# Stick-breaking attention: order of the projections, delays of copies, engine of the low parts, and place of the returns

## The chip, the cores and the metric

The kernel runs on one core of one Trainium2 chip. The core has five engines that each work through their own list of instructions in order: TensorE (PE) multiplies matrices, VectorE (DVE) and ScalarE (ACT) work on whole tiles, GpSimd (POOL) does the same and also issues DMAs here, and SyncE (SP) only issues DMAs. The metric is the time of one execution on the device in microseconds (us), smaller is better. Two kernels are compared by the median of several runs.

## The reference

One sequence of 1024 tokens, 1024 channels wide, in float32, passes two layers. Layer 0 mixes tokens with a gated linear recurrence, layer 1 with stick-breaking attention; a SwiGLU feed-forward follows each, with RMSNorm ahead of every part. The change lies in the attention of layer 1, 16 heads of 64 channels:

```
qkv = x @ w_qkv                                # (S, 3, 16, 64)
z = q @ k.T / 8                                # per head
log_fail = where(s < t, log_sigmoid(-z), 0)
suffix = cumsum(log_fail, reverse) - log_fail
weights = where(s < t, exp(log_sigmoid(z) + suffix), 0)
o = weights @ v
out = concat(o) @ w_o
```

So a query gives each earlier key a share of what the keys between the two have left over.

## The kernel before

Float32 products are made from two parts: a tile is split in a high part in a shorter format (a copy on ACT) and a low part, the difference (a subtraction on DVE or POOL), and `mm3` (lines 142 to 145) multiplies high by high, high by low and low by high.

Attention is lines 1473 to 1887. Heads go in eight pairs `q`, since two heads fill 128 partitions. For each pair the generator `qkv_steps` (line 1562) makes three projections, `which` 0, 1 and 2 for queries, keys and values, each in two halves `n` of 512 tokens. A half is eight steps of three matmuls, so a pair takes 48 steps. `next_weights` (line 1547) splits the weights of the projection after the present one, and `column_norms` (line 1525) finds scale factors `sv` and `av_` from the value weights, the last two operations of which are on POOL (lines 1541 and 1542).

`evacuate` (line 1589) takes a finished half out of its PSUM bank. Queries: a copy on ACT into `two`, a subtraction for the low part, and four DMAs from POOL (`spread`) that lay the parts out per head in `Q`. Keys: a multiplication on DVE into `t`, then the same, four DMAs into `KK`. Values: a product (line 1599) and a difference `t` (line 1601) on DVE, then `high` on ACT (line 1619) and `low` on DVE (line 1606) into `vx`, and two transposing DMAs from SP into `VV`. Differences of neighbouring values are used because the weights are kept as running products.

The scores of a head are made in twelve chunks, eight on the diagonal and four off it (`chunk_list`, line 1658). `z_part` multiplies, with two score banks in `psZ`; `z_rest` takes the sigmoid on ACT (line 1680); `scan` forms the running product on DVE (line 1687 on the diagonal, line 1690 off it, where it reads two inputs). The four chunks off the diagonal go through `turn_weights` (line 1694): a copy on ACT (line 1697) and a subtraction on POOL (line 1698) make the two f16 parts in `wx`, and a DMA from SP transposes them into `T`, tile name `wt`. The weights on the diagonal are instead transposed on PE (`t_part`) and split by `t_split` (lines 1721 and 1722). `av_part` multiplies weights and values in twelve units a head, one key block each.

After the last unit of a half, `gather`, `add_v` (on POOL, line 1751, except for the last pair) and `parts` bring a pair's outputs to `oo` and split them. They go to DRAM (`store`), because the tiles `xh` and `xl` still hold the projections' input. When the projections are done, `bring_back` (line 1512) loads them into `xh` and `xl` with DMAs from POOL, and the output projection (`ob`, by `out_fill`) begins among the last units.

The order of the work is written out by hand. A loop over `u` from -10 to 191 (line 1842) walks the units. In each, it first does what stands in `soon` (by `due`), then a chunk's scores, the weights of the chunk before (`turning`), the unit itself, one task from `later`, and two projection steps from `fill`. 42 steps are made ahead of the loop (AHEAD is 8), and in eight units of the last quarter only one step is made:

```
slower = range(132, 132 + 4 * AHEAD, 4)
...
                if u >= -2:
                    for _ in range(1 if u in slower else 2):
                        next(fill, None)
```

A function put in `soon` runs at the start of the next unit; there is no longer delay than that, only chains of functions that each put the next one in. The projections end at unit 164. The first twelve returns are issued in the low part of the last pair's first half of values, the other fourteen at the end of `all_fill` (line 1786).

Of the kernel before, what the change touches and what calls it, by code (L numbers as in the profile page):

```python
# [14 lines left out]
ALU = mybir.AluOpType  # L15
PSUM = bass.MemoryType.PSUM

P = 128
S = 1024
D = 1024  # L20
# [14 lines left out]
def trunk(  # L35
# [93 lines left out]
    def cols(w, c0, n=P):  # L129
        return w[:, c0 : c0 + n].rearrange("(k p) c -> p k c", p=P)  # L130
# [1357 lines left out]
    with ExitStack() as st:  # L1488
# [27 lines left out]


        def load_link(i):
            q, which = divmod(i, 3)
            if q < NP:  # L1520
                raws[i] = load_raw(cols(w_qkv, which * D + q * P), (ND,))
            else:
                mix[0].load(which)

        def column_norms(raw, q):
# [3 lines left out]
            def sums():  # L1529
                n_ps = psZ.tile([P, NB], F32, tag="z", name="n_ps")[:, 0:1]  # L1530
                for k in range(ND):
                    nc.tensor.matmul(
                        n_ps, lhsT=sq[:, k], rhs=g2[:, k : k + 1], start=k == 0, stop=k == ND - 1
                    )

                n2, h = (ap.tile([P, 1], t, tag=x, name=x, bufs=2) for x, t in (("n2", F32), ("nh", I32)))
                sv[q], av_[q] = (ap.tile([P, 1], I32, tag=x, name=x, bufs=3) for x in ("sv", "av"))
                nc.vector.tensor_scalar(n2, n_ps, 1e-30, 2.0, op0=ALU.max, op1=ALU.mult)
                one = float(1 << 23)
                nc.vector.tensor_single_scalar(h, n2.bitcast(I32), 24, op=ALU.logical_shift_right)  # L1540
                nc.gpsimd.tensor_scalar(sv[q], h, -one, 213 * one, op0=ALU.mult, op1=ALU.add)
                nc.gpsimd.tensor_scalar(av_[q], h, one, 41 * one, op0=ALU.mult, op1=ALU.add)

# [18 lines left out]
        def qkv_steps(q):  # L1562
            for which in range(3):
# [12 lines left out]
                for n in range(NH):  # L1576
                    pool, tag = (psZ, "z") if (q, which) == (0, 0) else (psQ, "qk")
                    ps = pool.tile([P, NB], F32, tag=tag, name="qk_ps")
                    for i, k in enumerate(ks):
                        mm3(ps, w[0][:, k], w[1][:, k], xh[k][n], xl[k][n], i == 0, i == ND - 1)  # L1580
                        if i < ND - 1:
                            yield
                    ev = evacuate(q, which, n, ps)
                    next(ev)
# [4 lines left out]
        def evacuate(q, which, n, ps):  # L1589
            full = lambda tag, m: [ap.tile([P, m, S], F32R, tag=tag, name=tag, bufs=4 if m == 1 else 3) for _ in range(2)]  # L1590
            cs = slice(n * NB, (n + 1) * NB)
            if which == 2:
# [12 lines left out]
                def low():  # L1605
# [3 lines left out]
                    for hx, a in enumerate((top, bot)):  # L1609
# [4 lines left out]
                        )  # L1614
                    if q == NP - 1 and n == 0:
                        bring_back(*((p, 0) for p in range(NP - 2)))

                def high():
                    nc.scalar.activation(vx[:, :, 0], t3, AF.Copy, scale=1 / UP)
                    soon.append(low)  # L1620

                soon.append(high)
                return
# [11 lines left out]
            def low():  # L1635
                nc.vector.tensor_sub(two[:, 1], t, f32(two)[:, 0])
                soon.append(spread)

# [7 lines left out]
            else:  # L1646
# [4 lines left out]
                yield  # L1651
                nc.scalar.copy(two[:, 0], t)
                soon.append(low)

# [39 lines left out]
        def turn_weights(q, hx, j, ci, c0, c1, diag):  # L1694
            F = W[q, hx, j, ci].rearrange("p (b c) -> p b c", c=P)
            wx = ap.tile([P, 4, 2, P], F16, tag="wx", name="wx", bufs=3)
            nc.scalar.copy(wx[:, :, 0], F)
            nc.gpsimd.tensor_sub(wx[:, :, 1], F, wx[:, :, 0])
            if j == 4:
# [27 lines left out]
        def av_part(tht, q, hx, G, kb, first, last):  # L1727
# [25 lines left out]
            def parts():  # L1753
# [9 lines left out]
                else:  # L1763
# [6 lines left out]

                    soon.append(store)

# [6 lines left out]
        units = [u for q, hx in heads for u in unit_list(q, hx)]  # L1779
        LEAD, AHEAD = 10, 8  # L1780

        def all_fill():
            yield from first
            for q in range(1, NP):
                yield from qkv_steps(q)
            bring_back((NP - 2, 0), *((p, 1) for p in range(NP - 2)))

# [21 lines left out]
        with tc.manual_schedule(engines={E.PE, E.Activation, E.DVE, E.Pool, E.SP}):  # L1809
# [11 lines left out]
            def due():  # L1821
                now = soon[:]
                soon.clear()
                for task in now:
                    task()

# [8 lines left out]
            gains = [len(units) - x for x in (31, 29, 27)]  # L1835
            slower = range(132, 132 + 4 * AHEAD, 4)

# [4 lines left out]
            for u in range(-LEAD, len(units)):  # L1842
# [28 lines left out]
                if u >= -2:  # L1871
                    for _ in range(1 if u in slower else 2):
                        next(fill, None)
# [60 lines left out]
```

## Time and profile before

| | |
|---|---|
| median of 3 runs | 2181.56 us (2178.86 to 2181.8) |
| the profiled execution | 2182.57 us |
| its span in the trace | 2179.8 us |
| mean granted clock of TensorE | 0.992 |
| attention in the trace | about 966 to 1460 us |
| DMA traffic over the span | 315.47 MB |

The span runs from the first to the last record of the trace; the profiled execution's own time has a little around it. In the lines of the profile, L1698 is line 1698 of the kernel. `out<-in` gives the tiles by their names in the program. A row of a timeline has the start, the duration, the engine, the line, the operation, its tiles and shapes, how many were merged, and in brackets how long the engine stood idle before it and who ended that wait. A wait line has the waiting engine and line, the one waited for, the total, the number of times and the longest. PEclk is the clock granted to TensorE, 1.00 at full speed. A busy time can hold time in which the instruction was held up.

### The profile page before, as it was taken

What the parts mean: (1) busy time and instruction counts of PE and PEld (TensorE: products, weight loads), DVE (VectorE), ACT (ScalarE), POOL (GpSimd) and SP (SyncE); (2) the same over time, 40 slices, a digit from 0 to 9 for tenths busy, and PEclk for the clock granted to TensorE, in tenths of its full rate; (3) what the DMA queues carried; (4) which work ended last, traced back from release to release, by engine and by line L of the source; (5) the groups of instructions that cost most, each with busy time, mean ns of one, the idle gap of its engine ahead of it and who ended that gap; (6) DMA issues with size and microseconds to landing.
All of it is one profiled execution on the core that took longest, in us unless ns stands there. A gap on an engine that the chain in (4) does not pass through costs nothing.

```text
span 2179.8 us, 28179 instructions
## 1 busy us (share of the span) xinstructions
PE 2137.5 (98%) x10158; PEld 1747.9 (80%) x10158; DVE 1769.7 (81%) x2543; ACT 1133.0 (52%) x1838; POOL 315.9 (14%) x346
## 2 busy tenths in 40 slices
PE   8999999999999999999999999889999999999998
PEld 7888888888888888887777777668888888888887
DVE  7888778888888887887888788866888888888886
ACT  6667445443444544555655555543544444454556
POOL 1222020000000000013444444531000000000002
PEclk9999999999999999999999999989999999999999
DMA  7111422344445864446676656873133444587452
GB/s 233 49 49 39 161 88 73 105 126 160 136 156 200 268 218 124 150 129 149 138 155 138 129 134 141 205 213 124 58 108 120 154 141 153 171 275 237 137 154 91
DMA packets 380844, 315.47 MB, mean 145 GB/s; under 512 B 101272, under 2 KB 296992, under 8 KB 380704
## 3 DMA queue, kind: packets, MB, share of 16 engines
q1 hardware_dynamic: 368192, 274.60, 42.2%
q0 software_dynamic: 12352, 38.81, 7.0%
q8 instruction: 79, 1.29, 0.2%
q14 instruction: 61, 0.50, 0.1%
q10 hardware_dynamic: 160, 0.27, 0.0%
HBM read 184.09 MB, written 83.36 MB: 123 GB/s over the span
## 4 chain that ended last, share of the span: by engine, by line
PE 90%; DVE 4%; issue 2%; DMA 2%; ACT 2%; POOL 1%; SPq 0%; DVEq 0%; ACTq 0%; POOLq 0%
PE p_ps L143 17%; PE p_ps L145 17%; PE p_ps L144 17%; PE qk_ps L143 3%; PE qk_ps L144 3%; PE qk_ps L145 3%; PE a_ps L144 3%; PE a_ps L145 3%; PE a_ps L143 3%; PE ob_ps L145 3%; PE ob_ps L143 2%; PE ob_ps L144 2%; PE av_ps L1735 2%; PE i_ps L145 1%; PE i_ps L144 1%
## 5 line engine op out<-in xcount | busy, mean ns | idle before, releaser
L143 PE MATMUL p_ps<-vh,wbh 128*128 128x512 f32 x524 | 204.9, 391 | 0.0
L144 PE MATMUL p_ps<-vl,wbh 128*128 128x512 f32 x524 | 204.5, 390 | 0.0
L145 PE MATMUL p_ps<-vh,wbl 128*128 128x512 f32 x524 | 204.0, 389 | 0.2 <-DVE wbl L726 0.2
L143 PE MATMUL p_ps<-vh,wch 128*128 128x512 f32 x524 | 204.2, 390 | 0.0
L145 PE MATMUL p_ps<-vh,wcl 128*128 128x512 f32 x524 | 204.1, 389 | 0.0
L144 PE MATMUL p_ps<-vl,wch 128*128 128x512 f32 x524 | 203.9, 389 | 0.0
L722 ACT CAST wbh<-sb 128x1024 fp32r<-128x1024 f32 (+2 forms) x69 | 69.6, 1009 | 192.6 <-DVE sb L702 192.6
L1680 ACT ACTIVATE w<-z_ps,rs 128x128 f32<-128x128 f32 (+1 forms) x192 | 110.1, 581 | 99.1 <-PE z_ps L1668 86.7
L143 PE MATMUL p_ps<-vh,wah 128*128 128x512 f32 x396 | 154.0, 389 | 0.0
L144 PE MATMUL p_ps<-vl,wah 128*128 128x512 f32 x396 | 154.0, 389 | 0.0
L145 PE MATMUL p_ps<-vh,wal 128*128 128x512 f32 x396 | 154.0, 389 | 0.0
L218 POOL TENSOR_TENSOR acc<-acc,rbc 128x512 f32<-128x512 f32 x30 | 40.6, 1352 | 766.8 <-ACT rbc L217 766.8
L1687 DVE TENSOR_TENSOR_SCAN w<-w,unit 128x128 f32<-128x128 f32 (+3 forms) x128 | 117.3, 923 | 21.9 <-ACT w L1680 21.8
L145 PEld LDWEIGHTS p_ps<-vh,wbl 128*128 128x128 f32 x524 | 98.4, 188 | 21.6 <-DVE wbl L726 0.7
L145 PEld LDWEIGHTS p_ps<-vh,wcl 128*128 128x128 f32 x524 | 98.4, 188 | 21.0 <-DVE wcl L736 0.6
L143 PEld LDWEIGHTS p_ps<-vh,wch 128*128 128x128 f32 x524 | 98.4, 188 | 20.5 <-ACT tb L1181 0.2
L144 PEld LDWEIGHTS p_ps<-vl,wch 128*128 128x128 f32 x524 | 98.4, 188 | 20.4
L143 PEld LDWEIGHTS p_ps<-vh,wbh 128*128 128x128 f32 x524 | 98.6, 188 | 19.8 <-ACT U L1181 0.4
L144 PEld LDWEIGHTS p_ps<-vl,wbh 128*128 128x128 f32 x524 | 98.6, 188 | 18.5
L143 PE MATMUL qk_ps<-vh,whi 128*128 128x512 f32 x264 | 113.2, 429 | 0.0
L1722 DVE TENSOR_TENSOR tl<-wt_ps,th 128x512 f16<-128x512 f32 (+3 forms) x128 | 56.6, 483 | 61.6 <-ACT th L1721 61.6
L144 PE MATMUL qk_ps<-vl,whi 128*128 128x512 f32 x264 | 104.6, 396 | 0.0
(411 smaller groups left out, 6073.7 us busy)
## 6 DMA issues: line engine op xcount, KB each, us to landing
raw<-in_ffn_w_in SPq DMA_DIRECT2D x88, 512.0 KB, 4.1
vl<-pd SPq DMA_DIRECT2D x128, 256.0 KB, 3.7
pd<-U SPq DMA_DIRECT2D x90, 256.0 KB, 2.3
kk<-two POOLq DMA_DIRECT2D x64, 256.0 KB, 4.6
raw<-in_ffn_w_out SPq DMA_DIRECT2D x56, 256.0 KB, 3.6
raw<-in_attn_w_qkv SPq DMA_DIRECT2D x24, 512.0 KB, 5.9
h<-hd SPq DMA_DIRECT2D x32, 256.0 KB, 5.5
hd<-h SPq DMA_DIRECT2D x32, 256.0 KB, 2.0
```

Source lines behind the costliest of these rows:

```text
L143: nc.tensor.matmul(ps, lhsT=wh, rhs=mh, start=first, stop=False, **kw)
L144: nc.tensor.matmul(ps, lhsT=wh, rhs=ml, start=False, stop=False, **kw)
L145: nc.tensor.matmul(ps, lhsT=wl, rhs=mh, start=False, stop=last, **kw)
L218: (eng or nc.gpsimd).tensor_add(acc[n], acc[n], sq)
L722: nc.scalar.copy(self.full(self.wb), self.full(self.sb))
L1680: nc.scalar.activation(F, ps[:, 0:n], AF.Sigmoid, scale=rs[:, j : j + 1])
L1687: nc.vector.tensor_tensor_scan(rev, rev, unit[:, NB - n :][:, ::-1], 0.0, op0=ALU.mult, op1=ALU.add)
L1722: nc.vector.tensor_sub(tl[:, q0:], tp[:, q0:], th[:, q0:])
L1735: nc.tensor.matmul(ps[:, q0:], lhsT=VV[q][:, hx, kb], rhs=t[:, q0:], start=first and x == 0, stop=last and x == 1)
```

## The change

From the second pair on, a pair's projections come in the order keys, queries, values (`kind`). `stage(task, steps)` puts a task into `soon` with a delay in units, and `due` counts it down. The keys' copy on ACT comes one unit later, the values' copy two units after their difference is formed, and the two POOL operations for `sv` and `av_` two units after the sums. In `turn_weights` the subtraction goes from POOL to DVE. The returns are taken out of `all_fill`: the first twelve are issued one unit after the low part of the first half of the last values, the other fourteen two units after that of the second half. AHEAD is 4, so 38 steps are made ahead of the loop, and `slower` is gone; the projections end at unit 162.

```diff
+        def kind(q, i):
+            return i if q == 0 else (1, 0, 2)[i]
+
+        def stage(task, steps=1):
+            soon.append([steps, task])
...
-                raws[i] = load_raw(cols(w_qkv, which * D + q * P), (ND,))
+                raws[i] = load_raw(cols(w_qkv, kind(q, which) * D + q * P), (ND,))
...
-                nc.gpsimd.tensor_scalar(sv[q], h, -one, 213 * one, op0=ALU.mult, op1=ALU.add)
-                nc.gpsimd.tensor_scalar(av_[q], h, one, 41 * one, op0=ALU.mult, op1=ALU.add)
+
+                def factors():
+                    nc.gpsimd.tensor_scalar(sv[q], h, -one, 213 * one, op0=ALU.mult, op1=ALU.add)
+                    nc.gpsimd.tensor_scalar(av_[q], h, one, 41 * one, op0=ALU.mult, op1=ALU.add)
+
+                stage(factors, 2)
...
-                    ev = evacuate(q, which, n, ps)
+                    ev = evacuate(q, kind(q, which), n, ps)
...
-                    if q == NP - 1 and n == 0:
-                        bring_back(*((p, 0) for p in range(NP - 2)))
+                    if q == NP - 1:
+                        back = [(p, n) for p in range(NP - 2)]
+                        stage(lambda: bring_back(*([(NP - 2, 0)] * n + back)), 1 + n)
...
                     nc.scalar.activation(vx[:, :, 0], t3, AF.Copy, scale=1 / UP)
-                    soon.append(low)
-
-                soon.append(high)
+                    stage(low)
+
+                stage(high, 2)
...
-                nc.scalar.copy(two[:, 0], t)
-                soon.append(low)
+
+                def high():
+                    nc.scalar.copy(two[:, 0], t)
+                    stage(low)
+
+                stage(high)
...
-            nc.gpsimd.tensor_sub(wx[:, :, 1], F, wx[:, :, 0])
+            nc.vector.tensor_sub(wx[:, :, 1], F, wx[:, :, 0])
...
-        LEAD, AHEAD = 10, 8
+        LEAD, AHEAD = 10, 4
...
-            bring_back((NP - 2, 0), *((p, 1) for p in range(NP - 2)))
...
-                for task in now:
-                    task()
+                for steps, task in now:
+                    if steps > 1:
+                        stage(task, steps - 1)
+                    else:
+                        task()
...
-            slower = range(132, 132 + 4 * AHEAD, 4)
...
-                    for _ in range(1 if u in slower else 2):
+                    for _ in range(2):
```

More of the change, by code (lines that the diff above doesn't have):

```diff
@@ L1636, in low @@
                 nc.vector.tensor_sub(two[:, 1], t, f32(two)[:, 0])
-                soon.append(spread)
+                stage(spread)
             if which == 0:
@@ L1769, in store @@
                         nc.gpsimd.dma_start(od[q, G][1], o)
-                    soon.append(store)
+                    stage(store)
             later.insert(0, gather)
```

## The prediction

> **What bounds the kernel now.** I read the page's busy times first, then the same by stage, then the waits of TensorE (PE) in one stage, then the timelines around two of those waits.
>
> ```profile
> PE 2137.5 (98%) x10158; PEld 1747.9 (80%) x10158; DVE 1769.7 (81%) x2543; ACT 1133.0 (52%) x1838; POOL 315.9 (14%) x346
> ```
>
> ```profile
> 0.00:966.00 966.00, 958.44 (x4428) 799.34 (x4429) 796.03 (x1130) 505.18 (x728) 66.10 (x39) 1.00 0.43 138
> 966.00:1460.00 494.00, 464.77 (x2350) 349.69 (x2349) 389.98 (x537) 278.55 (x548) 222.68 (x287) 0.97 0.67 150
> 1460.00:2179.80 719.80, 714.28 (x3383) 598.88 (x3381) 583.71 (x876) 349.28 (x563) 27.14 (x20) 1.00 0.46 150
> ```
>
> The windows' columns are stretch, length, busy time of PE, PEld, DVE (VectorE), ACT (ScalarE), POOL (GpSimd), then granted clock, DMA share and GB/s. PE is the bound everywhere, and the change touches only the middle row, attention: there PE is idle for 494.00 - 464.77 = 29.2 us and runs at a mean clock of 0.97. No PE work is added or removed, so the most that can come back is that idle time and what the clock takes. The waits of PE by releaser, up to 1398 us and behind it:
>
> ```profile
> PE z_ps L1667 <- ACT w L1680: 9.6, 7, 2.9
> PE av_ps L1735 <- DVE tl L1722: 1.9, 6, 0.4
> PE av_ps L1735 <- ACT th L1721: 1.5, 4, 0.4
> ...
> PE av_ps L1735 <- DMA wt<-wx: 0.5, 1, 0.5
> ```
>
> ```profile
> PE av_ps L1735 <- DMA v<-vx: 8.0, 1, 8.0
> PE z_ps L1667 <- ACT w L1680: 3.5, 1, 3.5
> PE z_ps L1667 <- DMA kk<-two: 2.3, 1, 2.3
> PE av_ps L1735 <- ACT th L1721: 0.7, 1, 0.7
> ```
>
> So 13.5 us are small waits that come back once per pair of heads, and 14.5 us are three large ones in the last 60 us. The granted clock falls in six stretches:
>
> ```profile
> 1220.40:1223.80 3.40, 3.40 (x12) 2.65 (x11) 3.40 (x8) 1.32 (x4) 0.00 (x0) 0.56 0.52 101
> 1278.50:1281.80 3.30, 2.85 (x9) 1.92 (x9) 3.06 (x6) 2.56 (x7) 0.96 (x1) 0.55 0.36 70
> 1336.50:1343.20 6.70, 5.50 (x14) 3.89 (x15) 4.74 (x10) 4.75 (x11) 1.16 (x1) 0.53 0.40 76
> 1397.90:1401.30 3.40, 2.84 (x10) 2.36 (x11) 3.29 (x5) 0.74 (x2) 3.16 (x5) 0.56 1.05 218
> 1415.00:1421.80 6.80, 4.87 (x13) 3.55 (x14) 3.79 (x7) 4.97 (x12) 3.60 (x7) 0.53 0.91 275
> 1428.70:1438.80 10.10, 4.37 (x14) 2.85 (x15) 7.58 (x8) 3.28 (x7) 3.12 (x3) 0.52 0.77 163
> ```
>
> PE was busy 11.75 us in the first three and 12.1 us in the last three; at about half speed, half of that is lost: 5.9 and 6.0 us. All that can be won is 13.5 + 14.5 + 5.9 + 6.0 = 40 us, 1.8% of the span. Each such stretch follows a wait of PE, so I take the lost clock to go with the waits.
>
> **The wait of each pair.** From ACT's, PE's, DVE's and POOL's timelines:
>
> ```profile
> 1276.83 0.63 ACT L1619 ACTIVATE vx<-t 128x512 f16<-128x512 f32 x1 [3.19 <-DVE t L1601]
> 1277.77 0.45 PE L1667 MATMUL z_ps<-kk,q 128*128 128x384 f32 x1 [1.42 <-ACT w L1680]
> ```
>
> ```profile
> 1266.13 1.27 DVE L1690 TENSOR_TENSOR_SCAN w<-w,w 128x512 f32<-128x512 f32 x1
> 1269.78 2.63 DVE L1690 TENSOR_TENSOR_SCAN w<-w,w 128x512 f32<-128x512 f32 x1
> 1273.57 2.04 DVE L1690 TENSOR_TENSOR_SCAN w<-w,w 128x512 f32<-128x512 f32 x1
> 1276.12 0.68 DVE L1601 TENSOR_TENSOR t<-vt 128x512 f32<-128x512 f32 x1
> ```
>
> ```profile
> 1267.72 2.40 POOL L1633 DMA_DIRECT2D kk<-two  x4
> 1270.13 3.24 POOL L1698 TENSOR_TENSOR wx<-w,wx 128x512 f16<-128x512 f32 x2
> 1273.37 1.16 POOL L1698 TENSOR_TENSOR wx<-w,wx 128x512 f16<-128x512 f32 x1
> ```
>
> ACT stands at the copy of V's high part because DVE has not yet formed t; the sigmoid that frees the score bank is queued behind that copy; PE waits for the sigmoid. DVE is late because V is evacuated among the four scans of the chunks off the diagonal, and two of these took 2.63 and 2.04 us instead of 1.27, just while POOL formed low parts of the weights.
>
> **Part by part.**
>
> *Low parts to DVE (L1698).* 64 subtractions leave POOL, eight in each pair of heads.
>
> ```profile
> 1100.00:1158.50 58.50, 55.80 (x288) 41.94 (x288) 48.32 (x66) 34.62 (x69) 26.46 (x33) 1.00 0.66 145
> ```
>
> ```profile
> L1690 DVE TENSOR_TENSOR_SCAN w<-w,w 128x512 f32<-128x512 f32 x8 | 12.6, 1573 | 0.0
> L1606 DVE SCALAR_TENSOR_TENSOR vx<-t,vx 128x512 f16<-128x512 f32 x2 | 1.4, 676 | 0.0
> ```
>
> No row shows the subtraction on DVE; the nearest is L1606, with the same strided f16 output and two inputs in SBUF: 676 ns, so 8 x 0.676 = 5.4 us a pair. Against it, the eight scans should fall from 12.6 to 8 x 1.27 = 10.2 us: -2.4. Bounds for the net cost on DVE: +0.6 us a pair (the other operations beside POOL are relieved by as much again) to +5.4 (nothing is relieved). I take +3.0, since the long scans stand exactly beside POOL's rows: 51.3 us in a pair that PE alone fills for 55.8. In the burst of four scans the sum is 4 x 0.68 = 2.7 added and 1.36 + 0.77 = 2.1 removed, about even. A unit (a key block; 24 a pair) is 58.5 / 24 = 2.44 us, and the subtraction sits one unit behind its scan. At even units it stands ahead of the subtraction tl (L1722), where DVE now waits for ACT; so part of it costs nothing, and without that cover it costs 0.68.
>
> The transposes wt<-wx on SP come earlier. ACT's copy of the next weights does not pass POOL's DMA issues any more.
>
> *Keys first, copies later.* Each third of a pair's projection is 16 steps, eight units. K comes eight units earlier, Q eight later, V's evacuation two units later in the burst's cycle, out of the four scans. V's copy on ACT is issued two units after t instead of one or less: the 3.19 us in front of it should go, and with it the wait of z for w. What is late next on ACT is the copy L1697, which waits for each scan; it has one unit of cover, 2.44 us, and the score banks give another. The K tiles have three buffers for two per pair; the new K goes into the buffer of the head whose last scores were made one unit before, so POOL's four kk issues wait for little. Q's transfers leave some six units (14 us) before use. The factors sv, two units later on POOL, are still about two units ahead of V's evacuation: nothing, or 2.44 us per unit by which they come late.
>
> *AHEAD 4 instead of 8, `slower` gone.* Four steps move from before the loop into it, and the projections end at unit 162 instead of 164. PE work is the same. At the start, scores come four steps earlier while K is a step later; the cover is PE's own projections; if it fails, at most one landing is exposed:
>
> ```profile
> kk<-two POOLq DMA_DIRECT2D x64, 256.0 KB, 4.6
> ```
>
> I count 0, range 0 to +4.6. Near the end the K of the last pair comes some eight units earlier, so the wait of 2.3 us goes, with half of the 2.84 us run slowly in that stretch: -3.7.
>
> *Outputs back behind the last values.*
>
> ```profile
> 1414.81 0.63 ACT L1619 ACTIVATE vx<-t 128x512 f16<-128x512 f32 x1 [5.21 <-DMA v<-vx]
> 1426.85 0.55 POOL L1515 DMA_DIRECT2D xg<-odl  x1 [0.20 <-DVE tl L1722]
> 1427.41 3.37 POOL L1698 TENSOR_TENSOR wx<-w,wx 128x512 f16<-128x512 f32 x3
> 1411.99 19.23 SPq L1701 DMA_TRANSPOSE wt<-wx  x3
> 1431.31 2.62 SPq L1610 DMA_TRANSPOSE v<-vx  x2
> 1427.21 6.02 DVE L1687 TENSOR_TENSOR_SCAN w<-w,unit 128x512 f32<-128x512 f32 x2
> ```
>
> Today SP waits 19 us for low parts that POOL forms only after it has issued the returns (last one at 1426.85), and V's last transposes stand behind them on SP; PE waits 8.0 us. With the subtraction on DVE and the returns of the second half issued two steps behind V's low part, both causes go. What remains is the tail itself, from the old end of the projections to the end of attention:
>
> ```profile
> 1409.00:1458.00 49.00, 36.42 (x174) 25.34 (x173) 34.61 (x40) 22.65 (x47) 21.97 (x26) 0.83 0.72 187
> DVE tl L1722 <- ACT th L1721: 13.1, 8, 4.5
> ```
>
> Without the slow clock PE needs 36.4 - 4.6 = 31.8 us there. DVE needs 34.6 + 8 x 0.68 - 4.4 (the two scans of 6.02, elsewhere 1.65 together) - 1.4 = 34.2, plus about 6 of the 13.1 us for ACT, which are not due to the stalls: about 41. DVE bounds the tail, which gives 8 us of the possible 17. The returns still pass POOL ahead of one addition (L1751), whose result ACT waits for; that is in the 41.
>
> *Sum* against the profiled execution, 2182.57 us (2179.8 and 2.8 around it, 1.0 above the median of 2181.56): pair waits -10.5 (of 13.5; I leave 3 for waits behind a fuller DVE), their clock -5.9, K -3.7, tail -8. Together -28.1: 2154.5, or about **2154** beside the median.
>
> One rule of the Trainium skill speaks of another cause. "TensorE: Matmul & The Clock Gate", What's actually happening, says that the clock halves after at least one idle window of about 3.4 us. The trace does not bear it out: ahead of the stretch at 1278.5 us PE had waited 1.42 us at once (row above), not a whole window. Were it the whole rule, the first three slow stretches would not come from these waits, as in rival (c).
>
> **The rivals.**
>
> (a) *DVE becomes the bound; slower.* For it: DVE has 48.32 of 58.50 us already. If the long scans have another cause than POOL, a burst takes 2.7 us more, and the chain scan, copy, sigmoid passes it on: 7 pairs x 2.7 = 19 us, and a slow stretch (1.7 us) in four pairs that have none: +26, less K and tail, 11.7: about 2197. It decides where the lag in a burst exceeds a unit, 2.44 us. Against it: scans that run without POOL's subtractions beside them take 1.27. "Perfetto Trace Analysis", Optimizing Scalar/DVE Operations, in the Trainium skill also says that work may be moved off a saturated VectorE, even to GpSimd, which is this change reversed; 83% is not saturated, so the trace does not bear it out yet.
>
> (b) *The pair's wait stays*, because the burst itself and not V's copy is late: only K and the tail are won, 2182.6 - 11.7 = 2171. For it: ACT also waits for scans at L1697 today.
>
> (c) *The slow stretches stay*: the first three have a cause of their own, other than the waits ahead of them. 2154 + 5.9 = 2160. Against it: each follows a wait, and the stage before, without waits, has clock 1.00.
>
> (d) *Nothing to be seen*: the returns' DMAs still delay V's transposes and DVE's load takes the rest: about 2181.
>
> **How the numbers follow.** Forecast 2154 (2143 to 2165) 0.64; (a) 0.14; (b) 0.14; (c) 0.04; (d) 0.04. A measurement here can tell about 0.2%, 4.4 us, from no change: faster 0.64 + 0.14 + 0.04 = 0.82, same 0.04, slower 0.14. The range runs from 2143, nearly all of the 40 us, over (c) and (b) with some waits added, to 2178, and leaves (a) and (d) out, 0.18.
>
> **What would show it.** Right: scans L1690 all near 1.3 us; wx<-w,wx on DVE at about 0.68; no wait of 3 us at L1619; PE's z waiting for w under 4 us in all; v<-vx absent from PE's waits; clock 1.00 up to the end of the projections. Wrong: DVE above 53 us in a pair, ACT waiting at L1697 for scans by more than 1 us each, or z waiting for w in every pair as before.

## The result, and the profile after

The changed kernel takes 2190.75 us (median of 5 runs, 2187.32 to 2192.54) against 2181.56: ratio 1.0044, interval 1.0029 to 1.0058. It is slower by about 9 us; 2154 was forecast, with a range of 2143 to 2178. The profiled execution took 2187.32 us and is the fastest of the five; its span is 2185.5. The two traces therefore differ by 5.7 us only, and the stages below account for these. The page's busy times, and two stretches of attention cut at the same place of the work in both kernels, first of the changed kernel and then of the one before (columns as in the prediction):

```profile
PE 2132.9 (98%) x10158; PEld 1743.8 (80%) x10158; DVE 1780.7 (81%) x2607; ACT 1130.6 (52%) x1838; POOL 233.7 (11%) x282
```

```profile
966.00:1395.50 429.50, 411.06 (x2132) 312.96 (x2132) 358.05 (x544) 248.26 (x491) 118.78 (x190) 1.00 0.72 143
1395.50:1466.10 70.60, 48.58 (x217) 32.26 (x217) 42.89 (x58) 27.46 (x55) 20.96 (x32) 0.78 0.88 194
```

```profile
966.00:1397.40 431.40, 415.80 (x2125) 315.56 (x2123) 345.29 (x486) 250.69 (x492) 192.53 (x247) 0.98 0.65 142
1397.40:1460.50 63.10, 49.47 (x227) 34.53 (x228) 44.73 (x53) 28.30 (x56) 30.15 (x40) 0.84 0.82 213
```

The cut is the `gather` that ends the last but one pair's first half, and the end is the last `gather` of all. By DVE's timeline these stand, with two gathers four pairs apart ahead of them, at

```profile
1095.78 0.66 DVE L1762 TENSOR_TENSOR oo<-av_ps,oo 64x512 f32<-64x512 f32 x1
1326.14 0.65 DVE L1762 TENSOR_TENSOR oo<-av_ps,oo 64x512 f32<-64x512 f32 x1
1395.49 0.69 DVE L1762 TENSOR_TENSOR oo<-av_ps,oo 64x512 f32<-64x512 f32 x1
1466.14 0.69 DVE L1762 TENSOR_TENSOR oo<-av_ps,oo 64x512 f32<-64x512 f32 x1 [2.49 <-ACT oo L1761]
```

in the changed kernel, and in the kernel before at

```profile
1095.51 0.66 DVE L1747 TENSOR_TENSOR oo<-av_ps,oo 64x512 f32<-64x512 f32 x1
1331.30 0.65 DVE L1747 TENSOR_TENSOR oo<-av_ps,oo 64x512 f32<-64x512 f32 x1
1397.37 0.69 DVE L1747 TENSOR_TENSOR oo<-av_ps,oo 64x512 f32<-64x512 f32 x1
1460.46 0.69 DVE L1747 TENSOR_TENSOR oo<-av_ps,oo 64x512 f32<-64x512 f32 x1 [2.45 <-ACT oo L1746]
```

So up to the cut the change is 1.9 us ahead, and the tail then takes 70.65 us instead of 63.09, 7.6 more; behind it nothing differs (719.3 and 719.4 us). Four pairs take 230.4 us instead of 235.8; part of that is lost again between the second gather shown and the cut, 69.4 us instead of 66.1. In the first stretch PE's busy time fell by 4.7 us, since its clock went from 0.98 to 1.00, but its idle time rose, from 431.40 - 415.80 = 15.6 us to 18.4. PE's waits up to 1398 us in the changed kernel show why:

```profile
PE av_ps L1750 <- DMA wt<-wx: 9.5, 6, 2.9
PE av_ps L1750 <- DVE tl L1737: 4.0, 7, 0.6
PE av_ps L1750 <- ACT th L1736: 2.7, 6, 1.4
```

The wait of z for the sigmoid, 9.6 us before, is gone. Waits of the second product for the transposed weights, 0.5 us before, have taken its place. In the tail three rows of PE's timeline hold nearly all of the idle time, and ACT's, SP's and POOL's say what stands behind them:

```profile
1412.93 0.80 PE L1682 MATMUL z_ps<-kk,q 128*128 128x512 f32 x1 [10.59 <-ACT w L1695]
1437.20 0.80 PE L1682 MATMUL z_ps<-kk,q 128*128 128x512 f32 x1 [9.13 <-ACT w L1695]
1443.22 1.03 PE L1750 MATMUL av_ps<-wt,v 128*128 128x512 f16 x2 [1.96 <-DMA wt<-wx]
```

```profile
1411.67 0.63 ACT L1630 ACTIVATE vx<-t 128x512 f16<-128x512 f32 x1 [10.56 <-DMA v<-vx]
1436.07 0.72 ACT L1773 ACTIVATE vh<-oo,av 128x512 fp32r<-128x512 f32 x1 [9.62 <-POOL oo L1766]
```

```profile
1399.27 2.52 SPq L1620 DMA_TRANSPOSE v<-vx  x2
```

```profile
1398.28 0.57 POOL L1514 DMA_DIRECT2D vh<-odh  x1
...
1434.37 0.55 POOL L1515 DMA_DIRECT2D xg<-odl  x1 [5.32 <-issue]
1434.93 1.10 POOL L1766 TENSOR_TENSOR oo<-oo,vt 128x512 f32<-128x512 f32 x1
```

The first stall: the last values' second high part (L1630) is written where the first half's transposes still read, for `vx` has one buffer. They were issued from 1399.27 on, one microsecond after the first of twelve returns, and ACT could write at 1411.67. The sigmoid is behind this copy, and z behind the sigmoid. The second: the sigmoid stands behind `parts` (L1773), which needs POOL's addition (L1766), and that stands behind fourteen returns, the last of which POOL could issue only at 1434.37. The DMA queues from 1400 to 1406 us (packets, MB, share of the 16 engines) show what the transposes met:

```profile
q0 software_dynamic: 376, 1.25, 102.7%
q1 hardware_dynamic: 752, 0.18, 14.9%
```

q0 carries GpSimd's DMAs, q1 SyncE's. A packet of the returns has 1.25 MB / 376 = 3.3 KB, one of the transposes 240 bytes. The Trainium skill's page "DMA: Bandwidth & Descriptors", Queues, rings and completion order, says that a DMA engine takes turns between its queues packet by packet. The counts here, two small packets to each large one, fit such turns, but they do not show the order of the packets, nor that the page counts packets as the profile does. The transposes moved a seventh of the returns' bytes in this time, and landed 9.3 us after their issue.

### The profile page after: what moved, and what is told of

Its sections match the earlier page's. It is cut to its first block, busy times and chain, and to the rows that moved or that the text cites. A ratio compares the mean times of both kernels' runs of the same rounds, so it can differ in the third digit from the quotient of the medians.

```text
span 2185.5 us, 28142 instructions
## 1 busy us (share of the span) xinstructions
PE 2132.9 (98%) x10158; PEld 1743.8 (80%) x10158; DVE 1780.7 (81%) x2607; ACT 1130.6 (52%) x1838; POOL 233.7 (11%) x282
## 4 chain that ended last, share of the span: by engine, by line
PE 86%; DMA 5%; DVE 5%; ACT 2%; issue 2%; SPq 0%; DVEq 0%; ACTq 0%
PE p_ps L143 17%; PE p_ps L144 17%; PE p_ps L145 17%; DMA wt<-wx 3%; PE a_ps L144 3%; PE a_ps L145 3%; PE a_ps L143 3%; PE ob_ps L143 2%; PE ob_ps L145 2%; PE ob_ps L144 2%; PE qk_ps L143 2%; PE qk_ps L145 2%; PE qk_ps L144 2%; PE av_ps L1750 2%; DMA v<-vx 2%
## 5 line engine op out<-in xcount | busy, mean ns | idle before, releaser
L1702 DVE TENSOR_TENSOR_SCAN w<-w,unit 128x128 f32<-128x128 f32 (+3 forms) x128 | 104.2, 820 | 39.6 <-ACT w L1695 39.4
L145 PE MATMUL qk_ps<-vh,wlo 128*128 128x512 f32 x264 | 103.6, 392 | 0.0
```

Source lines behind the costliest of these rows:

```text
L145: nc.tensor.matmul(ps, lhsT=wl, rhs=mh, start=False, stop=last, **kw)
L1702: nc.vector.tensor_tensor_scan(rev, rev, unit[:, NB - n :][:, ::-1], 0.0, op0=ALU.mult, op1=ALU.add)
```

## The experiments

Theory 1: the loss lies in the tail, where the returns keep the last transposes and POOL's addition back. The rivals: VectorE's load (theory 2), the returns' new place or the keys' transfers (theory 3; the keys' part is called theory 4 later on). Each ratio is to executions of the kernel before made beside that run, whose medians were 2180.05 to 2181.92 us. Line numbers shift by a few in each kernel.

### Which part of the change loses

**a_only**, the kernel before with the subtraction on DVE alone:

```diff
-            nc.gpsimd.tensor_sub(wx[:, :, 1], F, wx[:, :, 0])
+            nc.vector.tensor_sub(wx[:, :, 1], F, wx[:, :, 0])
```

> The kernel before with one part of the change: the low parts of the weights off the diagonal are formed on VectorE. Theory 1 (the change loses its time in the last 60 us only, where ScalarE stands behind the transposes of the last values and GpSimd's addition stands behind the returns; the load on VectorE is not the cause): faster than before, 2163 to 2177 us, the 8.0 us wait for v<-vx gone or small, the scans L1690 near 1.3 us. Theory 2 (VectorE's added load makes the change slow): slower than before, 2185 to 2192 us.

Measured 2200.52 us, ratio 1.0086 (1.0073 to 1.0099): slower than the whole change, and missed by both theories. PE's waits from 1040 to 1340 us begin with

```profile
PE av_ps L1735 <- DMA wt<-wx: 9.4, 4, 3.2
```

and the landings there (median, last column) are

```profile
kk<-two POOLq DMA_DIRECT2D x40, 256.0 KB, 7.4
```

where the kernel before has 4.7. The subtraction on POOL stood behind the keys' four DMA issues (rows at 1267.72 and 1270.13 in the prediction), and so the transposes left after the keys. On DVE nothing holds them, and both are under way together. The larger share of the loss lies in the tail, though. By the same gathers this kernel is 5.4 us behind at the cut, and its tail takes 77.7 us, 14.6 more than before, with the two waits of the changed kernel (z behind ACT, 21.5 us in two; ACT behind the values' transposes 12.6 and behind POOL's addition 11.1). So the tail's loss needs neither the new order nor the returns' new place. **without_a**, the change with the subtraction left on POOL (the reverse edit):

> The changed kernel with the low parts back on GpSimd; order, delays and returns as changed. Theory 1: still slow, 2186 to 2200 us, since values' transposes and returns still meet and GpSimd has more ahead of its addition. Theory 2 (VectorE's load): back to 2175 to 2182 us.

2209.82 us, ratio 1.0132 (1.0119 to 1.0145), above both ranges. The subtraction on DVE costs 18.6 us in the old order and saves 19.1 in the new one. Each half alone loses more than both, so the change cannot be priced as a sum of its edits. In this kernel PE waits in every pair for the high parts `th` from ACT:

```profile
PE av_ps L1750 <- ACT th L1736: 10.1, 10, 1.8
```

Here the loss lies ahead of the tail: 23.9 us at the cut, then a tail of 65.0 us, 1.9 more than before. From 1040 to 1340 us PE also waits for `wt`, 7.6 us in four.

**old_returns**, the changed kernel with the returns put back to about their old places:

```diff
-                    if q == NP - 1:
-                        back = [(p, n) for p in range(NP - 2)]
-                        stage(lambda: bring_back(*([(NP - 2, 0)] * n + back)), 1 + n)
+                    if q == NP - 1 and n == 0:
+                        bring_back(*((p, 0) for p in range(NP - 2)))
...
+            stage(lambda: bring_back((NP - 2, 0), *((p, 1) for p in range(NP - 2))), 2)
```

> The changed kernel with the returns about where the kernel before has them: the first twelve with the low part of the first half of the last values, one unit earlier than changed; the other fourteen two units after the projections' end, three units earlier. Theory 1 (the two meet in either place, because nothing makes GpSimd's issues wait for the transposes): within 4 us of the changed kernel, 2186 to 2194 us. Theory 3 (the new place of the returns is what costs): 2172 to 2181 us.

2194.45 us, ratio 1.0065 (1.0052 to 1.0078), within theory 1's 4 us and 0.45 above its range. The new place gains 3.7 us; PE's waits in the tail are of the same kind in both (z behind ACT, 17.6 us in two, and 8.0 for `wt`; in the changed kernel 19.7 and 2.0).

### Is it the returns

**no_returns**, the changed kernel without the 26 loads:

```diff
-            for q, n in which:
-                nc.gpsimd.dma_start(f32(xh[q][n]), od[q, n][0])
-                nc.gpsimd.dma_start(f32(xl[q][n]), od[q, n][1])
+            pass
```

> The changed kernel without the 26 returns: the outputs that went to DRAM are not loaded back, so the output projection multiplies what the tiles held before. Theory 1 (the returns take the DMA engines and GpSimd's queue while ScalarE waits): both z waits (10.6 and 9.1 us) go, 2160 to 2172 us. Rival (the tail is bound by VectorE and the waits would come back elsewhere): 2180 us or more.

2169.24 us, ratio 0.9955 (0.9942 to 0.9967): 21.5 us less than the changed kernel, within theory 1's range. One wait of the two goes; of the other, for `vx`, this much remains without any return:

```profile
PE z_ps L1680 <- ACT w L1693: 4.2, 1, 4.2
```

**freed_tail** keeps the returns and takes their two victims away: a buffer of its own for the last values' second half, and the last but one addition on DVE:

```diff
+                if (q, n) == (NP - 1, 1):
+                    spare = ap.tile([P, 2, NB], F32R, tag="two", name="two", bufs=2)
+                    vx = spare[:, 0].bitcast(F16).rearrange("p (b h c) -> p b h c", b=4, h=2)
+                else:
+                    vx = ap.tile([P, 4, 2, P], F16, tag="vx", name="vx", bufs=1)
...
-                eng = nc.vector if q == NP - 1 else nc.gpsimd
+                eng = nc.vector if q + G >= NP - 1 else nc.gpsimd
```

> The changed kernel with two waits of the tail taken away: the second half of the last pair's values goes into a buffer of its own (a free tile of the keys), so ScalarE need not wait for the first half's transposes; and the addition of the last outputs but one is on VectorE, so ScalarE need not wait for GpSimd behind its returns. Theory 1: the z waits of 10.6 and 9.1 us go, some of it comes back at the transposed weights: 2168 to 2180 us. Theory 2: 2187 us or more, since VectorE has as much to do.

2180.22 us, ratio 0.9994 (0.9984 to 1.0004), 0.2 above theory 1's range. Both waits of z are gone, but ACT now waits at the next place, for a buffer `wx` that a late transpose holds:

```profile
ACT wx L1716 <- DMA wt<-wx: 11.5, 1, 11.5
```

**before_freed**, the kernel before with the same two edits:

> The kernel before with the same two reliefs of the tail alone (buffer of its own for the last values, last-but-one addition on VectorE), nothing of the change. If the change's order is worth the 5 us that its pairs gained, and only the tail spoilt it: 2175 to 2184, near or above the changed kernel with the same reliefs (2180.2). Rival, the reliefs help the old order as much as the new (10 us): 2168 to 2174, and then the change loses at an equal tail too.

2181.72 us, ratio 1.0 (0.9991 to 1.0009): the reliefs bring the old order nothing. With the same reliefs the two orders can't be told apart (2180.2 and 2181.7).

### Their place, their spacing, their queue

**early_returns**, freed_tail with the first twelve returns issued as soon as the projections of the last values' first half end (at 1387 us instead of 1403), and the last four additions on DVE:

> freed_tail with the first twelve returns issued as soon as the first half of the last values is out of its bank, three units ahead of that half's transposes instead of one unit behind, and the last four additions of outputs on VectorE. Theory 1: the transposes of the last values meet less traffic, the 11.5 us in which ScalarE waits there for a wx buffer shrinks to under 5: 2166 to 2176 us. Rival (the DMA engines are full for the whole tail, the place of the returns only moves the wait): 2178 to 2184 us.

2189.11 us, ratio 1.004 (1.0026 to 1.0053). Missed: PE's tail now begins with

```profile
PE av_ps L1755 <- DMA wt<-wx: 16.9, 1, 16.9
```

The burst met the weights' transposes instead of the values'. **early_late** adds the keys' spread one unit later (`stage(spread, 1 + which)`):

> early_returns with the keys' DMAs one unit later, as in late_keys. If both theories hold, the two gains add: 2160 to 2172 us, clearly below the kernel before (2181.9). If neither holds: 2178 to 2185 us.

2188.62 us, ratio 1.0038 (1.0026 to 1.0051), above both ranges, with a wait of 18.0 us at the same line: nothing gained (late_keys, below, shows why the delay changes nothing). **paced** is freed_tail with two return DMAs per unit instead of a burst:

```diff
+            owed.extend((q, n, x) for q, n in which for x in range(2))
+
+        def bring_some(m):
+            for q, n, x in owed[:m]:
+                nc.gpsimd.dma_start(f32((xh, xl)[x][q][n]), od[q, n][x])
+            del owed[:m]
...
+                bring_some(2)
```

> The changed kernel with both reliefs of the tail (last values' low and high parts in a buffer of their own, last-but-one addition on VectorE; 2180.2 us as measured), and the returns issued two transfers per unit instead of twelve and fourteen at once, from the same units on. Theory 1, the burst of returns takes the DMA engines from the transposes for some ten us at a stretch: spread out, the landings of wt come back to under 8 us, and with them the waits of 11.5 us on ScalarE and the waits for returned tiles; 2165 to 2177. Rival, the DMA traffic of the tail as a whole is the bound, however it is spread: the same waits stand at other places, 2178 to 2186.

2193.2 us, ratio 1.0053 (1.004 to 1.0067), above both ranges. **spread** begins earlier, with one DMA per unit, and spreads the first steps of the output projection too:

> As the paced one, but the returns begin a unit before the last values' first half is staged and go one transfer per unit until the projections' end, two from then on; the early steps of the output projection are spread one per unit over the tail, and the last four additions run on VectorE. Theory 1: with about 1 transfer of 256 KB per 2.4 us the engines are never full; no wait of PE over 3 us in the last 60 us; 2162 to 2174. Rival (total traffic): 2178 to 2190, with landings of wt over 10 us still there.

2187.05 us, ratio 1.0034 (1.0019 to 1.0049), one wait of 12.2 us for wt. This fits the rival, but POOL's timeline in spread shows that the spacing never took place:

```profile
1389.19 0.55 POOL L1519 DMA_DIRECT2D xg<-odl  x1
1402.07 0.56 POOL L1793 DMA_DIRECT2D odh<-oh  x1 [12.33 <-ACT oh L1783]
1403.98 0.54 POOL L1794 DMA_DIRECT2D odl<-oo  x1 [1.36 <-DVE oo L1784]
1404.59 0.55 POOL L1519 DMA_DIRECT2D vh<-odh  x1
```

The first four returns left at once; then POOL stood 12.33 us at the store of a pair's outputs, and the next thirteen followed within 8 us. In paced, too, thirteen left within 9.3 us behind such a store. The two runs decide nothing on the spacing. **act_queue** is freed_tail with the returns issued by ACT (`nc.scalar.dma_start`):

> The changed kernel with both reliefs, and the 26 returns issued by ScalarE on its own DMA queue instead of by GpSimd. Theory 1a, the transposes lose to GpSimd's queue in particular (it has 74 to 103% of the engines while they have 7 to 15%): on a queue like their own they share evenly, landings of wt stay under 9 us, 2165 to 2177. Theory 1b, any transfer of 256 KB in numbers crowds the transposes out: landings of 10 to 20 us stay, 2178 to 2188. ScalarE pays for the issues in either case, at most some 26 times 0.1 us, and if it stands at a full queue, more: over 2188.

2193.75 us, ratio 1.006 (1.0047 to 1.0073). The transposes of wt land within 10.1 us instead of 14.3, not under 9, and ACT pays, as the expectation's last sentence feared: an issue shows 0.33 to 0.78 us there, not 0.1, with gaps of up to some 5 us between two. It issued twelve returns from 1399.92 on and came to its sigmoid at

```profile
1412.08 0.58 ACT L1699 ACTIVATE w<-z_ps,rs 128x384 f32<-128x384 f32 x1 [11.69 <-DMA xg<-odl]
```

The other fourteen kept it 13.69 us.

**sp_paced** puts the returns on the transposes' own queue, in SyncE's list behind those of the unit, one per unit from the end of the first half's projections on. SyncE only issues DMAs, so it keeps the order of its list. From unit 172 on it is three in two units; the output projection's early steps are those of spread, and the reliefs those of freed_tail:

```diff
-                nc.gpsimd.dma_start(f32((xh, xl)[x][q][n]), od[q, n][x])
+                nc.sync.dma_start(f32((xh, xl)[x][q][n]), od[q, n][x])
...
+                bring_some(1 if u < last_two + 4 else 1 + u % 2)
```

> The changed kernel with the two reliefs of the tail; the returns are issued by SyncE, on the queue of the transposes, one per unit from the unit in which the projections of the last values' first half end, behind that unit's transposes (three in two units from unit 172 on), and the output projection's early steps go one per unit over the tail. Theory 1 in its first form, the returns hurt by coming in a burst of 12 to 14: no transpose stands behind more than one or two of them, landings of wt stay under 8 us, no wait of PE over 3 us in the last 60 us; 2163 to 2175. Rival, the traffic of the tail is too much in whatever order: 2178 to 2190, with waits of 10 us still there.

2179.26 us, ratio 0.9994 (0.9985 to 1.0002). The time misses theory 1's range and lies in the rival's, but what theory 1 says of the transposes holds: the landings of wt from 1395 to 1460 us (least, median, most) are

```profile
DMA to landing us min/median/max: 3.2/3.9/4.9
```

where the changed kernel has 18.8 for the most. PE's waits in the tail are now for the returned tiles themselves:

```profile
PE ob L144 <- DMA vl<-odl: 6.2, 3, 3.0
PE z_ps L1692 <- ACT w L1705: 2.5, 4, 1.6
PE ob L143 <- DMA vh<-odh: 1.9, 1, 1.9
```

On this queue the returns no longer delay the attention, but the last of them come late for the output projection. They are spaced only in SyncE's list: where it stands at a transpose whose input is not ready, the returns behind pile up, and eleven of them left within 5.3 us, from 1417.84 on. So it was not the spacing that helped.

### The waits in the pairs

**late_keys**, the changed kernel with the keys' spread one unit later in POOL's list (`stage(spread, 1 + which)`):

> The changed kernel with the keys' four DMAs (kk<-two) issued one unit later, behind the last transpose wt<-wx of a head. Theory 3 (in the pairs, PE waits for wt<-wx because the keys' megabyte now goes to the same DMA engines just ahead of these transposes): the waits of av for wt before 1380 us fall from 10.9 us in seven to under 4 us, the time to 2183 to 2187 us. Rival (VectorE forms the last low part too late, the DMA traffic does not matter): waits as before, 2189 to 2192 us.

2192.01 us, ratio 1.0057 (1.0044 to 1.0069): nothing gained, and PE's waits for wt are 9.5 us in five up to 1380 us. But the run tests nothing, since the transfers did not move:

```profile
1129.84 0.69 DVE L1647 TENSOR_TENSOR two<-t,two 128x512 fp32r<-128x512 f32 x1
1131.43 2.38 POOL L1644 DMA_DIRECT2D kk<-two  x4
```

They leave 1.59 us after DVE begins their low part, in the changed kernel 1.60 (1124.97 and 1126.57). POOL has no other instruction between the two places in its list, and issues them as soon as their input is there.

**same_keys** leaves the keys' transfers out from the third pair on:

```diff
-                        for half_ in (top, bot):
+                        for half_ in (top, bot) if q < 2 else ():
...
-                    KK[q] = full("kk", 2)
+                    KK[q] = full("kk", 2) if q < 2 else KK[1]
```

> The changed kernel, with the keys' transfers left out from the third pair of heads on (all later pairs are scored against the second pair's keys; the vector work on the keys stays). Theory 4, in the pairs the weights' transposes are late because they now leave together with the keys' transfers: PE's waits for wt in the pairs fall from about 1 us each to under 0.3, landings of wt to 3.2 us, and from the fifth gather of a pair to the twenty-first pass under 228 us instead of 230.4; tail as in the changed kernel; 2183 to 2189. Rival, other transfers (queries, raw weights, values) or SyncE's own order delay them: wt waits stay as they are, 2188 to 2192.

2181.9 us, ratio 1.0005 (0.9995 to 1.0015), 8.9 less than the changed kernel. Four pairs take 225.2 us (230.4 with the transfers), and PE's waits from 1040 to 1340 us hold no wt at all, against 4.8 us there in the changed kernel:

```profile
PE av_ps L1750 <- DVE tl L1737: 2.9, 5, 0.6
PE av_ps L1750 <- ACT th L1736: 1.4, 5, 0.3
```

**same_both** leaves the queries' out as well:

> As the last, with the queries' transfers left out as well. Theory 4 with the queries in it: the landings of wt fall further, waits of PE for wt near 0 in the pairs, 2181 to 2188. Rival: as the last, 2188 to 2192.

2183.66 us, ratio 1.0019 (1.0008 to 1.0029): no further gain, the keys are the ones that matter. **gaps** moves them instead of dropping them, the keys' first half three units later, the second half one, the queries' second half two:

```diff
-                stage(spread)
+                stage(spread, {(1, 0): 4, (1, 1): 2, (0, 1): 3}.get((which, n), 1) if q else 1)
```

> The changed kernel with the spreads of keys and queries moved into the gaps between the bursts of transposes: the first half of the keys three units later, the second half one, the second half of the queries two. Theory 4 (transposes and keys leave together): the waits for wt in the pairs go as they did without the keys' transfers; tail as in the changed kernel; 2180 to 2186. Rival, the transfers collide with something else there (raw weights, values), or the scores wait for the keys: 2187 to 2195.

2201.38 us, ratio 1.0091 (1.0077 to 1.0105). Missed: wt is gone from PE's waits from 1040 to 1340 us, as theory 4 had it, but its rival held on what comes instead, and the time lies above its range too. The first half's keys now do move, behind the stores of a pair's outputs in POOL's list and 8.56 us behind their low part. They hold the two buffers `two` until the queries' copy on ACT needs one, and z stands behind that:

```profile
ACT two L1654 <- DMA kk<-two: 29.6, 5, 6.1
```

```profile
PE z_ps L1682 <- ACT w L1695: 11.2, 5, 2.5
```

**gaps_sp** is the same on sp_paced:

> The version with SyncE issuing the returns between the transposes (2179.3 us) and the spreads moved into the gaps as in the other kernel. If the two causes are separate, the gains add: some 6 to 9 us less, 2169 to 2174, which beats both kernels. Rival: the spreads' gain is given back in the tail, where the DMA engines are full anyway: 2176 to 2181.

2187.12 us, ratio 1.0026 (1.0017 to 1.0035), above both ranges: 7.9 more than sp_paced, with the same wait (30.8 us in 5).

### A version that beats both

**best** is sp_paced with two returns per unit from unit 166 on, and the keys' first half two units later, the queries' second half two:

```diff
-                stage(spread)
+                stage(spread, {(1, 0): 3, (0, 1): 3}.get((which, n), 1) if q else 1)
...
-                bring_some(1 if u < last_two + 4 else 1 + u % 2)
+                bring_some(1 if u < last_two - 2 else 2)
```

> The version with SyncE issuing the returns between the transposes (2179.3 us), with the first half of the keys spread two units later instead of three, the second half where the change has it, the second half of the queries two units later; and the returns two per unit from unit 166 on. Theory 4 with a place for the keys: no wait of ScalarE for the shared buffer, waits for wt in the pairs under 0.3 us, the waits for returned tiles down from 8 us; 2166 to 2174, faster than both kernels. Rival, there is no free place: ScalarE still waits 1 to 4 us per pair for the buffer, or PE for wt; 2176 to 2186.

2171.72 us, ratio 0.996 (0.9948 to 0.9971): 9.5 us faster than the kernel before and 19 faster than the change. The gain is the tail's: from the cut to the last gather it takes 51.3 us (63.1 in the kernel before, 59.3 in sp_paced, 52.8 in no_returns). Some 7 us of small waits are all that PE has there, none for returned tiles, and the queue of the transposes carries nearly everything from 1395 to 1460 us:

```profile
PE z_ps L1692 <- ACT w L1705: 2.7, 4, 1.6
```

```profile
q1 hardware_dynamic: 23386, 16.34, 92.6%
```

Two per unit is again only the order of the list. By SyncE's timeline seventeen returns leave within 10 us,

```profile
1416.48 1.24 SPq L1726 DMA_TRANSPOSE wt<-wx  x1
1417.81 0.52 SPq L1519 DMA_DIRECT2D vl<-odl  x1
...
1427.62 0.32 SPq L1519 DMA_DIRECT2D xg<-odl  x1
1428.30 6.81 SPq L1726 DMA_TRANSPOSE wt<-wx  x3
```

a burst at least as dense as GpSimd's twelve in 11 us in the changed kernel. The transpose ahead of it lands in 4.0 us, those behind it in 6.6 at most.

In the pairs the expectation failed: PE still waits there for wt, from 1040 to 1340 us 5.2 us, and four pairs take 231.9. The delays of the spreads did nothing here: from 1040 to 1340 us POOL's operations come in the same order as in the changed kernel, and the keys leave 1.59 us behind their low part, as there. A place between this and gaps, behind the stores but early enough for the buffers, was not tried, nor was a third buffer.

## Why the prediction was wrong

**The low parts on DVE were priced rightly.** The row of 1100 to 1158.5 us has 51.73 us for DVE, where 51.3 was forecast:

```profile
1100.00:1158.50 58.50, 57.28 (x300) 42.95 (x299) 51.73 (x79) 34.82 (x70) 16.59 (x25) 1.00 0.73 150
```

From 1040 to 1340 us its groups by line (total, mean ns of one) are

```profile
L1705 DVE TENSOR_TENSOR_SCAN w<-w,w 128x512 f32<-128x512 f32 x40 | 55.2, 1380 | 0.3 <-ACT w L1695 0.3
L1713 DVE TENSOR_TENSOR wx<-w,wx 128x512 f16<-128x512 f32 x42 | 28.4, 677 | 2.8 <-ACT wx L1712 1.2
```

676 ns were taken from the neighbouring row, 677 came; the scans fell from 1573 to 1380 ns, not quite to 1270. POOL's subtraction did slow them: in the two pairs of kernels that differ by that line alone, a scan takes 1581 ns in the kernel before and 1276 in a_only, 1790 in without_a and 1380 in the change (1040 to 1340 us). That agrees with the Trainium skill, "SBUF — State Buffer", Who interferes with whom: an operation of VectorE with two inputs in SBUF contends with a GpSimd instruction that reads SBUF. Rival (a), DVE as the bound, gave the right sign for a wrong reason: PE's waits for DVE's `tl` rose by 2.1 us only, 1.9 to 4.0.

**The old wait of each pair and its clock went as forecast.** V's copy no longer waits 3.19 us for `t`, z waits no more, and the clock up to the cut is 1.00: 4.7 us of busy time against the forecast 5.9. The wait for K (2.3 us) went too, and near 1095 us the changed kernel is 0.3 us behind, so the earlier start (AHEAD) cost little. Rival (b) falls with the wait of z, rival (c) with the slow stretches.

**The step that failed in the pairs** is "pair waits -10.5 (of 13.5; I leave 3 for waits behind a fuller DVE)". Idle time up to the cut rose by 2.8 us instead. I had written "The transposes wt<-wx on SP come earlier" and given it no price: their new company was the keys' transfers, behind which POOL's list had kept them. same_keys shows that these make the waits, 5.2 us in four pairs, and gaps that they go when the keys leave later.

**The step that failed in the tail**, and turned the sign, is the term of -8 with its ground, "DVE bounds the tail, which gives 8 us of the possible 17". With K's -3.7 it stood for -11.7 behind the cut; 7.6 came on top instead. "Both causes go" held for what it named: SP no longer stands for POOL's low parts, and PE's 8.0 us for v<-vx are gone. But two other waits, in which ACT stands and z behind it, were taken to fit into the 41 us, and they grew. In the kernel before they were

```profile
1403.30 2.53 SPq L1610 DMA_TRANSPOSE v<-vx  x2
1431.86 0.72 ACT L1758 ACTIVATE vh<-oo,av 128x512 fp32r<-128x512 f32 x1 [5.10 <-POOL oo L1751]
```

and the row that I quoted, ACT's 5.21 us for v<-vx at 1414.81. There the transposes held `vx` for 11.5 us after their issue, beside the returns, and ACT came to its copy 6.3 us after it; now they hold it for 12.4 and ACT comes after 1.8, so the wait is 10.56. The addition on POOL, in the prediction "in the 41", kept ACT 5.10 us and now, behind fourteen returns, 9.62. no_returns shows the returns to be the cause (21.5 us, and all but 4.2 of the wait for `vx`), freed_tail the two places. sp_paced and best show that neither the traffic nor its coming in a burst is the cause as such, since as many returns, seventeen of them in as dense a burst, on the transposes' own queue and behind those that are due, delay nothing. That DVE is not the bound shows in best: 51.3 us where the forecast 41 of 49 would leave 55. Rival (d) had the mechanism of the returns, at no change and a chance of 0.04. In the sum for DVE, which gave the 41, the prediction does not say where its last 1.4 us come from.

**What stays open:** why without_a waits for `th` (ACT's copies ahead of it wait for scans that take 1790 ns there, which may be all); why the subtraction on DVE lengthens the tail in the old order too; and which of the differences of sp_paced from freed_tail, the queue, the earlier start or the output projection's later steps, is worth how much.

## What to carry to other kernels

When a step is moved to another engine, ask which order the old engine kept by being busy: here POOL's list had kept the weights' transposes behind the keys' transfers, and each half of the change alone cost 19 and 28 us, though the whole cost 9. Price an issue that comes earlier by what is on the DMA engines at that moment, read from the landings by tile, not by its queue alone. A delay written into the order of a list moves a transfer only if something that waits comes to stand ahead of it: look in the timeline whether it moved before judging the theory. And bulk transfers can stand behind the urgent small ones on the same queue, on an engine that only issues DMAs; here that took the tail's large waits away, while the attempts to space the transfers never took effect.

## What the runs showed of the hardware

A transpose of `wx` that lands in 3.2 us took up to 18.8 us beside fourteen 256 KB transfers of GpSimd (22.8 beside twelve in early_returns), and at most 6.6 us in best, where as many transfers stand on its own queue. An engine that issues many DMAs in a row comes late to its next work: GpSimd stood up to 5.32 us ahead of a return in the changed kernel, where the profile names no releaser, and ScalarE 11.69 and 13.69 us at twelve and fourteen returns (act_queue). A scan of VectorE with two inputs takes 1276 ns without GpSimd's subtractions beside it and 1581 with them (a_only and the kernel before).
